# 28 adaLN chunks move from TensorE to VectorE; cached keys, bias tables and the out-projection's residual are handled in another order

## The chip, the cores and the metric

One core of one Trainium2 chip runs the whole program. The time is device microseconds of one launch. TensorE (PE) has two clock levels, 2.4 and 1.2 GHz; the profile gives the granted clock as a share of the higher one. The other engines are VectorE (DVE), ScalarE (ACT), GpSimd (POOL) and SyncE (SP); every DMA of this program is issued from SP's queue, in the order written, and a transfer that must wait for a buffer holds up all that stand behind it.

## The reference

Two layers (DEPTH = 2) over 128 context tokens and 512 latent tokens, width 1024. All arithmetic is fp32.

```python
for l in range(DEPTH):
    sh1, sc1, g1, sh2, sc2, g2 = split(silu(cond) @ ada_w[l] + ada_b[l], 6)      # adaLN, one row for context, one for latents
    h   = x * (1 + sc1) + sh1
    mix = concat([diff_attention(h), neighbourhood_attention(h), mlstm(h)])       # parts a, b, c of one input projection
    x   = layer_norm(ALPHA * x + g1 * (mix @ w_out[l]))
    h   = x * (1 + sc2) + sh2
    x   = layer_norm(ALPHA * x + g2 * (square(relu(h @ w_mlp1[l])) @ w_mlp2[l]))
```

The attentions of the latents also read 256 cached keys and values per head; part b adds a relative-position bias table to its local scores. `cond` has two rows (context and latents), so the adaLN product is 2 x 1024 by 1024 x 6144 for each layer.

## The kernel before, in words

The 640 tokens are five tiles of 128 (tile 0 context, tiles 1 to 4 latents). An fp32 product is three TensorE matmuls of two-part splits (`mul3`, L98 to L100): high x high, low x high, high x low. A weight comes from memory 1 MB at a time into one of two `raw` buffers (L208); ACT makes the high part (L170) and DVE the low part (L117), in four pieces each, into the slots `wt0`, `wt1` and, in the MLP, a third one in `AK`.

The program is a list of Units. The weight transfers are issued in the order of first use, as far ahead as the two buffers allow; a Unit that needs a weight makes sure that its split has been issued. A scheduler then settles the order on each engine from the order of the list.

A layer is: c_proj and c_attn (mLSTM), b_proj and b_attn (neighbourhood attention), a_proj and a_attn (differential attention), woven with the out-projection (`out_units`: for each tile the contributions of parts b and c, `cb`, and later those of part a, `a`, each in two halves of 512 columns), the norm, `put_T` (transpose, modulate, split), and the MLP (`mlp_units`: 8 blocks c of 512 hidden columns; the list has the up units of block c and then the down units of block c-1, one for each tile, each of which adds 128x1024 sums to `Y` on DVE, L1416).

The adaLN product is made in chunks of 1 MB (256 output columns), 24 for each layer, which share the `raw` buffers with the weights but are not split: 8 matmuls with the conditioning as the stationary operand (L368), a copy by ACT, and two Units later a "pick" of the two rows out of four groups. For v = 0, 1, 3, 4 (shifts and scales, wanted per partition) the pick is two matmuls against `sel2` (L385); for v = 2, 5 (the gates, wanted as rows) it is a matmul with `selr` (L380), a DVE add of a bias row that has its own DMA, and a DMA to `s_gate`. Where the chunks stand:

```python
ada = self.ada_units(l, (2, 3, 4))                            # in the attention of both layers, 12 chunks each
...
spare = self.ada_units(l, (5,))                               # in the MLP: 4 chunks in both layers
if more:
    spare += self.ada_units(l + 1, (0, 1)) + [self.mod_unit(l + 1, 0)]    # and 8 more in the first
for c in range(1, NFF - 1):
    P_ += ups[c]
    P_ += weave(downs[c - 1], spare[:2] if c < NFF - 2 else spare)
```

In part b each head's `prep` (L887 to L897) loads queries and keys, 128 KB of cached keys (`ckf`, L891, one buffer), which ACT and DVE split (L892, L893), and a bias table (`rw`, L896, one buffer). In `out_units`, `cb` multiplies its sums by the gate row (L1278), loads the residual's half tile (`z1`, two buffers), scales it in the second layer (L1283, L1284) and adds it (L1285); `a` multiplies its own sums by the gate (L1291) and adds them (L1292).

Of the kernel before, what the change touches and what calls it, by code (L numbers as in the profile page):

```python
# [42 lines left out]
PACK = (("abT", (DEPTH, 48)), ("lnT", (DEPTH, 4, KT)), ("ident", (P,)), ("sel2", (2,)), ("selr", (32,)),  # L43
# [25 lines left out]
class Step:  # L69
# [61 lines left out]
    def w_src(self, k):  # L131
        kind, l, j = k
        d = self.d
        if kind == "ada":
            return d["ada"][l, j]
# [43 lines left out]
    def run(self, plan):  # L179
# [32 lines left out]
        def try_split(slack=0):  # L212
            while state["split"] < state["dma"] and order[state["split"]][0] == "ada":
                state["split"] += 1
# [23 lines left out]
        for i, u in enumerate(plan):  # L238
# [3 lines left out]
            for k in u.w:  # L242
# [6 lines left out]
                if k[0] != "ada":  # L249
# [12 lines left out]
            for k in u.w:  # L262
                if k[0] == "ada" and last[k] == i:
                    del self.raw[k]
# [21 lines left out]
    def setup(self):  # L286
# [30 lines left out]
        nc.vector.tensor_tensor(self.condS, self.condS, e, ALU.mult)  # L317

# [39 lines left out]
    def ada_units(self, l, vecs, own=None):  # L358
# [15 lines left out]
        def pick(v, q, part):  # L374
            po = self.mm("pick")
            if v in (2, 5):
                ab = self.adp.tile([2, CW], F32, name="abrow", bufs=1)
                off = v * D + q * CW
                nc.sync.dma_start(ab, self.d["ada_b"][l, off:off + CW].partition_broadcast(2))
                nc.tensor.matmul(po[:32, :CW], self.selr, part, start=True, stop=True)  # L380
                nc.vector.tensor_tensor(ab, po[:2, :CW], ab, ALU.add)
                nc.sync.dma_start(self.s_gate[l][v // 3][:, q * CW:(q + 1) * CW], ab)
            else:
                for b in range(2):
                    nc.tensor.matmul(po[:, 2 * b:2 * b + 2], part[:, b * P:(b + 1) * P], self.sel2,  # L385
                                     start=True, stop=True)
                c0 = v * KT + 2 * q
                nc.vector.tensor_tensor(
                    self.adaF[l][:, v, 2 * q:2 * q + 2, :], po[:, :4].rearrange("p (a b) -> p a b", b=2),
                    self.abT[:, l, c0:c0 + 2, None].to_broadcast([P, 2, 2]), ALU.add)  # L390
# [4 lines left out]
        return out  # L395

# [173 lines left out]
    def head_load(self, l, kind, h):  # L570
# [4 lines left out]
        k = self.hp.tile([P, NTOK + PAST], F32R, name="hk", tag="hk", bufs=2)  # L575
        for g in range(2):
            o = slice(64 * g, 64 * g + 64)
            nc.sync.dma_start(q[o].bitcast(F32), self.s_q[kind + "q"][l][f][rows])
            nc.sync.dma_start(k[o, :NTOK].bitcast(F32), self.s_q[kind + "k"][l][f][rows, g])
# [274 lines left out]
    def b_proj(self, l):  # L854
# [13 lines left out]
        u = self.proj_fm(l, 4, self.sink_fm(l, "bq"))  # L868
        u += self.proj_fm(l, 5, self.sink_fm(l, "bk"))
        u += self.proj_tm(l, 6, range(NT), sink_v)  # L870
        return u

    def b_attn(self, l):
# [14 lines left out]
        def prep(h):  # L888
            q, k = self.head_load(l, "b", h)
            ck = self.bw.tile([P, PAST], F32, name="ckf", tag="ckf", bufs=1)  # L890
            nc.sync.dma_start(ck, d["cbk"][l, :, h])  # L891
            nc.scalar.activation(k[:, NTOK:], ck, AF.Copy, scale=0.125)  # L892
            nc.vector.scalar_tensor_tensor(k[64:, NTOK:], ck[64:], 0.125, k[64:, NTOK:].bitcast(F32),  # L893
                                           op0=ALU.mult, op1=ALU.subtract)
            rw = self.bw.tile([P, 8, 48], F32, name="rw", tag="rw", bufs=1)
            nc.sync.dma_start(rw, d["rpbw"][l, h])  # L896
            bm = []  # L897
            for v in range(3):
                b = self.bw.tile([P, 8, 32], F32, name="bm", tag="bm", bufs=4)
                o = 16 + BLK_OFF[v]  # L900
                nc.gpsimd.tensor_tensor(b, rw[:, :, o:o + 32], self.nmask[:, v, None, :].to_broadcast([P, 8, 32]), ALU.add)
                bm.append(b)
            hold[h] = (q, k, bm)
            hold[h, "r"] = self.bw.tile([P, 5], F32, name="br", tag="br", bufs=2)

        def scores(h, c):
# [9 lines left out]
            else:  # L916
# [3 lines left out]
                kl = k[:, P:NTOK].rearrange("p (r w) -> p r w", r=8)[:, :, w]  # L920
                self.mul2(ps[:, :256], kl, qq, stack_stationary=False)
                self.mul2(ps[:, 256:], k[:, NTOK:], qq, stack_stationary=False)
# [64 lines left out]
    def a_proj(self, l):  # L987
        nc, d = self.nc, self.d

        def op():  # L990
# [9 lines left out]
            nc.sync.dma_start(self.AV[:, 0:2], d["cav"][l])  # L1000

        held = {}

        def cached(g):
            if g < 4:
# [485 lines left out]
    def layer(self, l):  # L1491
# [75 lines left out]
        if more:  # L1567
            spare += self.ada_units(l + 1, (0, 1)) + [self.mod_unit(l + 1, 0)]
# [155 lines left out]
```

## Time and profile before

| | us |
|---|---|
| median of 3 runs | 1877.81 (1877.62 to 1882.55) |
| the profiled execution, its own time | 1881.12 |
| its span in the profile | 1879.3 |
| PE / DVE / ACT / POOL busy | 1790.4 / 1083.5 / 724.3 / 100.4 |
| TensorE's granted clock, mean | 0.981 |

The profile shows one execution. Busy times say how loaded an engine is over the whole span; what a stage is worth is read from the windows of that stage, from the chain of waits in it, and from the single rows of the timeline.

### The profile page before, as it was taken

Reading aid. Unit: us, or ns where it says so; the run is one execution under the profiler, and the core shown is the slowest. Engines: PE = TensorE matmul, PEld = TensorE weight load, DVE = VectorE, ACT = ScalarE, POOL = GpSimd, SP = SyncE. Lnnn points to the kernel's source line nnn. Section 1 sums busy time; section 2 is a strip of 40 time slices with the busy share of each in tenths; the row PEclk is TensorE's granted clock in tenths of the full one; section 3 lists DMA queues with packets and bytes.
Section 4 is the critical chain, followed back from the end, with each engine's and each line's share of the span. In section 5 each row is a group of like instructions: output and inputs, shape, how many; then the busy total and the mean of one; then the engine's idle time right before and its main releaser. Section 6 shows DMA issues by size and latency. Waiting matters only on the chain.

```text
span 1879.3 us, 29111 instructions
## 1 busy us (share of the span) xinstructions
PE 1790.4 (95%) x11666; PEld 1607.1 (86%) x11666; DVE 1083.5 (58%) x2068; ACT 724.3 (39%) x1640; POOL 100.4 (5%) x153
## 2 busy tenths in 40 slices
PE   6999999998999999999999989988989999999996
PEld 4999888887888888888899988877879889998895
DVE  4755566787623343345777645677977134544477
ACT  3343235456533231232364423353566223322220
POOL 1111100000000000000010210000010000000001
PEclk9999999999999999999999989989999999999998
DMA  9555465321423332333336655461214224222221
GB/s 352 163 165 163 164 201 189 111 85 57 146 68 102 123 115 91 109 107 140 106 116 222 162 167 179 145 214 64 85 45 146 90 90 157 69 90 68 75 94 56
DMA packets 82712, 239.23 MB, mean 127 GB/s; under 512 B 31808, under 2 KB 44544, under 8 KB 63888
## 3 DMA queue, kind: packets, MB, share of 16 engines
q1 hardware_dynamic: 82576, 237.36, 38.2%
q8 instruction: 92, 1.51, 0.3%
q14 instruction: 44, 0.36, 0.1%
HBM read 210.78 MB, written 26.55 MB: 126 GB/s over the span
## 4 chain that ended last, share of the span: by engine, by line
PE 82%; DVE 9%; DMA 5%; ACT 2%; issue 1%; SPq 1%; POOL 0%; DVEq 0%; ACTq 0%
PE m L98 15%; PE m L99 15%; PE m L100 15%; PE ss L98 7%; PE ss L99 7%; PE ss L100 7%; PE ss L1115 1%; PE m L1145 1%; PE m L961 1%; PE m L368 1%; DVE wt L117 1%; DMA ada<-ada 1%; DVE anm L1118 1%; DMA z<-s_x 1%; PE mz L106 1%
## 5 line engine op out<-in xcount | busy, mean ns | idle before, releaser
L98 PE MATMUL m<-wt,Th 128*128 128x256 f32 (+2 forms) x864 | 274.8, 319 | 7.1 <-DVE Tl L1206 2.8
L99 PE MATMUL m<-wt,Th 128*128 128x256 f32 (+2 forms) x864 | 269.1, 312 | 0.0
L100 PE MATMUL m<-wt,Tl 128*128 128x256 f32 (+2 forms) x864 | 267.0, 311 | 0.0
L98 PE MATMUL m<-Th,AK 128*128 128x384 f32 (+1 forms) x736 | 229.3, 312 | 4.9 <-DVE Th L112 4.2
L99 PE MATMUL m<-Tl,AK 128*128 128x384 f32 (+1 forms) x736 | 229.1, 312 | 0.9 <-DVE Tl L117 0.9
L100 PE MATMUL m<-Th,AK 128*128 128x384 f32 (+1 forms) x736 | 225.9, 311 | 0.0
L170 ACT ACTIVATE wt<-raw 128x512 fp32r<-128x512 f32 x244 | 146.7, 627 | 149.3 <-PE ss L100 85.6
L117 DVE TENSOR_TENSOR wt<-raw,wt 128x512 fp32r<-128x512 f32 x244 | 162.3, 693 | 47.1 <-ACT wt L170 46.2
L98 PEld LDWEIGHTS m<-wt,Th 128*128 128x128 f32 x864 | 168.6, 195 | 22.4 <-issue 5.5
L100 PEld LDWEIGHTS m<-wt,Tl 128*128 128x128 f32 x864 | 167.4, 195 | 10.8 <-issue 3.1
L99 PEld LDWEIGHTS m<-wt,Th 128*128 128x128 f32 x864 | 169.0, 196 | 7.6 <-issue 1.7
L98 PE MATMUL m<-Th,wt 128*128 128x384 f32 (+1 forms) x536 | 166.4, 311 | 0.0
L100 PE MATMUL m<-Th,wt 128*128 128x384 f32 (+1 forms) x536 | 166.2, 310 | 0.0
L99 PE MATMUL m<-Tl,wt 128*128 128x384 f32 (+1 forms) x536 | 165.9, 310 | 0.0
L1416 DVE TENSOR_TENSOR Y<-ss,Y 128x1024 f32<-128x1024 f32 x60 | 73.2, 1223 | 156.8 <-PE ss L100 156.8
L1390 DVE SCALAR_TENSOR_TENSOR rl<-m,rl 128x384 f32<-128x384 f32 (+1 forms) x128 | 62.2, 488 | 164.5 <-ACT rl L1389 164.5
L98 PEld LDWEIGHTS m<-Th,AK 128*128 128x128 f32 x736 | 140.7, 191 | 8.8 <-DVE Th L112 4.7
L99 PEld LDWEIGHTS m<-Tl,AK 128*128 128x128 f32 x736 | 140.7, 191 | 3.7 <-issue 1.6
L100 PEld LDWEIGHTS m<-Th,AK 128*128 128x128 f32 x736 | 140.5, 191 | 1.0 <-issue 0.8
L98 PE MATMUL ss<-wt,hid 128*128 128x512 f32 x356 | 139.7, 395 | 0.0
L1389 ACT ACTIVATE rl<-m 128x384 f32<-128x384 f32 (+1 forms) x128 | 55.3, 434 | 218.8 <-PE m L100 216.1
L99 PE MATMUL ss<-wt,hid 128*128 128x512 f32 x356 | 138.8, 391 | 0.0
(705 smaller groups left out, 3554.4 us busy)
## 6 DMA issues: line engine op xcount, KB each, us to landing
raw<-w SPq DMA_DIRECT2D x64, 1024.0 KB
raw<-ada SPq DMA_DIRECT2D x40, 1024.0 KB
raw<-w_in SPq DMA_DIRECT2D x24, 1024.0 KB
ada<-ada SPq DMA_DIRECT2D x8, 1024.0 KB
raw<-w_out SPq DMA_DIRECT2D x8, 1024.0 KB
s_x<-Y SPq DMA_DIRECT2D x15, 512.0 KB
hq<-s_cq SPq DMA_DIRECT2D x16, 320.0 KB
nb<-s_nm SPq DMA_DIRECT2D x16, 320.0 KB
```

The costliest lines, as they stand in the source:

```text
L98: mt(out, a[0], b[0], start=first, stop=False)
L99: mt(out, a[0], b[1], start=False, stop=False)
L100: mt(out, a[1], b[0], start=False, stop=last)
L106: self.nc.tensor.matmul(out, a, b, start=first and i == 0, stop=last and i == 1)
L117: self.nc.vector.tensor_tensor(out, x, hi.bitcast(F32), ALU.subtract)
L170: self.nc.scalar.activation(hi, r, AF.Copy)
L368: nc.tensor.matmul(ps[32 * g:32 * g + 32, :CW], self.condS[:, kt, :], raw[:, kt, :], start=kt % 2 == 0, stop=kt % 2 == 1)
L961: nc.tensor.matmul(out[64 * i:64 * i + 64], w, rhs, start=b == 0, stop=b == nb - 1)
L1115: nc.tensor.matmul(ps[:, b, :384], qq[i], K[:, j, b * 384:b * 384 + 384], start=i == 0, stop=i == 1)
L1389: nc.scalar.activation(r[:, :n], ps[:, :n], AF.Relu)
L1390: nc.vector.scalar_tensor_tensor(r[:, :n], ps[:, :n], 0.0, r[:, :n], op0=ALU.max, op1=ALU.mult)
L1416: nc.vector.tensor_tensor(y, ps, y, ALU.add)
```

## The change

1. **Chunks.** 28 chunks, v = 5 of the first layer and all 24 of the second, are made on DVE during the first layer's MLP (`ada_dve`). Their weights come transposed (`adaT`, prepared in memory): 128 output columns on the partitions, the 1024 inputs along the row, two such blocks in 1 MB. The silu of the conditioning is broadcast to all partitions (`condB`). Four instructions for each chunk (two blocks by two rows of cond) multiply and sum along the row. One chunk stands behind each of 28 down units. The second layer's attention and MLP have no chunks left.
2. **Gates.** All picks go by `sel2`; a gate is turned into rows once for each v (two transposes, an ACT copy, a DMA; `gate_rows`).
3. **Part b.** The cached keys of all four heads are one transfer of 512 KB and one split at the start of b_proj; bias tables have two buffers and are loaded two heads ahead, the `bm` tiles six buffers instead of four.
4. **Part a.** `cak` has two buffers, loaded a step earlier.
5. **Out-projection.** `cb` only copies its sums into `Y` (ACT). `a` adds, multiplies by the gate and adds the residual, which comes as whole rows of 1024, one tile ahead.
6. **Copies.** The second half of the `aT` copies (32 of 128x384) and one cast of each `put_T` (15 of 128x512) go from DVE to ACT.
7. **Start.** The conditioning is also loaded as rows, put through silu and stored (`s_cond`).

```diff
+    def ada_dve(self, l, vecs):
+        nc = self.nc
+        def emit(v, q):
+            raw = self.raw[("adt", l, 4 * v + q)].rearrange("p (a b) -> p a b", b=D)
+            for b in range(2):
+                for j in range(2):
+                    x = self.mw.tile([P, D], F32, name="adx", tag="z2", bufs=2)
+                    nc.vector.scalar_tensor_tensor(x, raw[:, b], 1.0, self.condB[:, j], op0=ALU.mult, op1=ALU.mult,
+                                                   accum_out=self.adaF[l][:, v, 2 * q + b, j:j + 1])
+            if q == 3:
+                a = self.adaF[l][:, v]
+                nc.vector.tensor_tensor(a, a, self.abT[:, l, KT * v:KT * v + KT, None].to_broadcast([P, KT, 2]), ALU.add)
+                if v in (2, 5):
+                    self.gate_rows(l, v)
+        return [Unit(0, lambda v=v, q=q: emit(v, q), (("adt", l, 4 * v + q),), soft=True) for v in vecs for q in range(4)]
...
-        ada = self.ada_units(l, (2, 3, 4))
+        ada = self.ada_units(l, (2, 3, 4) if l == 0 else ())
...
-        spare = self.ada_units(l, (5,))
+        spare = []
         if more:
-            spare += self.ada_units(l + 1, (0, 1)) + [self.mod_unit(l + 1, 0)]
+            spare = self.ada_dve(l, (5,)) + self.ada_dve(l + 1, (0, 1)) + [self.mod_unit(l + 1, 0)]
+            spare += self.ada_dve(l + 1, range(2, 6))
         for c in range(1, NFF - 1):
             P_ += ups[c]
-            P_ += weave(downs[c - 1], spare[:2] if c < NFF - 2 else spare)
-            spare = spare[2:]
+            for x in downs[c - 1]:
+                P_ += [x] + spare[:1]
+                spare = spare[1:]
...
+            ck = self.hp.tile([P, H, PAST], F32, name="ckf", tag="ckf", bufs=1)
+            nc.sync.dma_start(ck, d["cbk"][l])
+            k = self.BK = self.hp.tile([P, H, PAST], F32R, name="BK", tag="BK", bufs=1)
+            nc.scalar.activation(k, ck, AF.Copy, scale=0.125)
+            nc.vector.scalar_tensor_tensor(k[64:], ck[64:], 0.125, k[64:].bitcast(F32), op0=ALU.mult, op1=ALU.subtract)
...
         def cb(t, n):
             ps = self.out_mm(l, t, 2, n)
+            nc.scalar.activation(self.Y[:, t, 512 * n:512 * n + 512], ps, AF.Copy)
...
-            nc.vector.tensor_tensor(f, ps, self.g1[min(t, 1)][:, cols], ALU.mult)
-            nc.vector.tensor_tensor(self.Y[:, t, cols], self.Y[:, t, cols], f, ALU.add)
+            v, y, z = nc.vector, self.Y[:, t, cols], res[t][:, cols]
+            v.tensor_tensor(y, ps, y, ALU.add)
+            v.tensor_tensor(y, y, self.g1[min(t, 1)][:, cols], ALU.mult)
+            v.scalar_tensor_tensor(y, z, ALPHA if l == 0 else 1.0, y, op0=ALU.mult, op1=ALU.add)
```

DVE's order at the end of a middle block of the first MLP (c = 2), from the second down unit's add to the split of the next block's first weight (`ss` are a down unit's sums; `AK` is the third weight slot, `m1` the first up unit's sums). Before:

```order
L1416 TENSOR_TENSOR Y_99<-ss_6218,Y_99 128x1024
L1416 TENSOR_TENSOR Y_99<-ss_6257,Y_99 128x1024
L1416 TENSOR_TENSOR Y_99<-ss_6283,Y_99 128x1024
L381 TENSOR_TENSOR abrow_6310<-m3_6309,abrow_6310 2x256
L117 TENSOR_TENSOR AK_1981<-raw_6255,AK_1981 128x512 x2
L1416 TENSOR_TENSOR Y_99<-ss_6315,Y_99 128x1024
L117 TENSOR_TENSOR AK_1981<-raw_6255,AK_1981 128x512 x2
L1390 SCALAR_TENSOR_TENSOR rl_6389<-m2_6364,rl_6389 128x384
```

After, from the fourth down unit's add on (a chunk's four instructions are on L426):

```order
L426 SCALAR_TENSOR_TENSOR adx_6361,adaF1_99<-raw_6297,condB_5222 128x1024
L1483 TENSOR_TENSOR Y_110<-ss_6299,Y_110 128x1024
L426 SCALAR_TENSOR_TENSOR adx_6363,adaF1_99<-raw_6297,condB_5222 128x1024
L426 SCALAR_TENSOR_TENSOR adx_6365,adaF1_99<-raw_6297,condB_5222 128x1024
L426 SCALAR_TENSOR_TENSOR adx_6367,adaF1_99<-raw_6297,condB_5222 128x1024
L1483 TENSOR_TENSOR Y_110<-ss_6335,Y_110 128x1024
L117 TENSOR_TENSOR AK_1999<-raw_6333,AK_1999 128x512 x4
L1457 SCALAR_TENSOR_TENSOR rl_6406<-m1_6381,rl_6406 128x384
```

The next block's weight was split with two pieces ahead of the last add and two behind it; now all four pieces stand behind the last add, and so behind every chunk instruction of the block.

SP's queue at the start of the second layer's part b. Before, the cached keys of head 0 and its bias table stand behind the read-back of the values (`Y<-s_bv1`):

```order
L866 DMA s_bv1_129<-vb_10534 128x256
L208 DMA raw_10621<-ada 128x2048
L885 DMA Y_99<-s_bv1_129 128x1x256 x4
L891 DMA ckf_10579<-cbk 128x256
L896 DMA rw_10583<-rpbw 128x384
L1000 DMA AV_10550<-cav 128x1024
```

After, they are in the queue before the first part of the mLSTM's queries is stored:

```order
L1511 DMA s_x1_118<-Y_110 128x1024 x2
L910 DMA ckf_9749<-cbk 128x1024
L926 DMA rw_9754<-rpbw 128x384
L926 DMA rw_9756<-rpbw 128x384
L210 DMA raw_9344<-w_in 128x2048
L605 DMA s_cq10_123<-st_9187 128x1280
```

Some 45 rows of the queue lie between their new place and the read-back of the values.

## Rows read from the trace of the kernel before

**Rows 1.** the profile page, busy time of each engine and share of the span

```profile
PE 1790.4 (95%) x11666; PEld 1607.1 (86%) x11666; DVE 1083.5 (58%) x2068; ACT 724.3 (39%) x1640; POOL 100.4 (5%) x153
```

**Rows 2.** windows: us, busy of PE, PEld, DVE, ACT, POOL, clock, DMA share, GB/s

```profile
500.00:960.00 460.00, 459.88 (x2688) 406.03 (x2688) 218.44 (x353) 147.98 (x297) 5.19 (x12) 1.00 0.32 109
1095.00:1135.00 40.00, 33.13 (x257) 31.36 (x256) 17.93 (x39) 9.60 (x22) 6.61 (x10) 0.87 0.57 183
1135.00:1250.00 115.00, 111.18 (x983) 96.24 (x981) 73.75 (x179) 48.67 (x122) 3.56 (x6) 0.98 0.55 176
1250.00:1335.00 85.00, 72.03 (x398) 60.93 (x398) 68.14 (x131) 35.94 (x91) 2.41 (x4) 0.94 0.36 118
1480.00:1840.00 360.00, 360.00 (x2015) 322.50 (x2015) 167.51 (x250) 107.94 (x206) 0.00 (x0) 1.00 0.27 93
```

**Rows 3.** timeline of PE, one chunk in the first MLP: start, us, instruction

```profile
546.99 0.39 PE L100 MATMUL ss<-wt,hid 128*128 128x512 f32 x1
547.31 1.09 PE L368 MATMUL m<-raw,condS 128*32 128x256 f32 x16
548.33 0.50 PE L98 MATMUL ss<-wt,hid 128*128 128x512 f32 x1
548.67 0.40 PE L99 MATMUL ss<-wt,hid 128*128 128x512 f32 x1
548.91 0.40 PE L100 MATMUL ss<-wt,hid 128*128 128x512 f32 x1
```

**Rows 4.** timeline of PE, one pick of a gate's rows

```profile
559.47 0.62 PE L380 MATMUL m<-adpart,pack 128*32 128x256 f32 x2
560.02 0.44 PE L98 MATMUL m<-Th,AK 128*128 128x384 f32 x1
560.30 0.34 PE L99 MATMUL m<-Tl,AK 128*128 128x384 f32 x1
```

**Rows 5.** timeline of PE, one pick per partition

```profile
749.29 0.50 PE L385 MATMUL m<-pack,adpart 128*128 128x2 f32 x4
749.65 0.36 PE L98 MATMUL m<-Th,AK 128*128 128x256 f32 x1
749.86 0.28 PE L99 MATMUL m<-Tl,AK 128*128 128x256 f32 x1
```

**Rows 6.** groups by line and form: busy us, mean ns, idle before

```profile
L1416 DVE TENSOR_TENSOR Y<-ss,Y 128x1024 f32<-128x1024 f32 x60 | 73.2, 1223 | 156.8 <-PE ss L100 156.8
L117 DVE TENSOR_TENSOR wt<-raw,wt 128x512 fp32r<-128x512 f32 x244 | 162.3, 693 | 47.1 <-ACT wt L170 46.2
L1436 DVE SCALAR_TENSOR_TENSOR x<-Y,mv,lnrows 128x1024 f32<-128x1024 f32 x4 | 5.1, 1277 | 0.0
L1285 DVE SCALAR_TENSOR_TENSOR Y<-z,Y 128x512 f32<-128x512 f32 x20 | 13.7, 683 | 0.0
```

**Rows 7.** timeline of ACT, the read of an accumulator behind its activation

```profile
1142.76 0.20 ACT L925 ACTIVATION_READ_ACCUMULATOR bp<-my,bnm 128x1 f32 x1
```

**Rows 8.** timeline of DVE, the last down unit's add of two MLP blocks

```profile
626.01 1.22 DVE L1416 TENSOR_TENSOR Y<-ss,Y 128x1024 f32<-128x1024 f32 x1
...
866.93 1.23 DVE L1416 TENSOR_TENSOR Y<-ss,Y 128x1024 f32<-128x1024 f32 x1
```

**Rows 9.** one weight transfer alone: its issue on SP, and the windows behind

```profile
607.92 0.33 SPq L208 DMA_DIRECT2D raw<-w  x1
...
612.00:613.00 1.00, 1.00 (x6) 0.83 (x5) 0.00 (x0) 0.00 (x0) 0.00 (x0) 1.00 0.04 16
```

**Rows 10.** chain of waits, second layer, start of part b

```profile
1098.20 6.29 DMA Y<-s_bv
...
1108.96 7.55 DMA ckf<-cbk
```

**Rows 11.** chain of waits, second layer, start of the out-projection

```profile
1247.42 12.13 DMA lnrows<-ln
...
1267.90 6.85 DMA z<-s_x
```

More of the change, by code (lines that the diff above doesn't have):

```diff
@@ L212, in try_split @@
         def try_split(slack=0):
-            while state["split"] < state["dma"] and order[state["split"]][0] == "ada":
+            while state["split"] < state["dma"] and order[state["split"]][0] in ("ada", "adt"):
                 state["split"] += 1
@@ L262, in run @@
             for k in u.w:
-                if k[0] == "ada" and last[k] == i:
+                if k[0] in ("ada", "adt") and last[k] == i:
                     del self.raw[k]
@@ L375, in pick @@
             po = self.mm("pick")
[L376 to L390, printed above, removed]
+            for b in range(2):
+                nc.tensor.matmul(po[:, 2 * b:2 * b + 2], part[:, b * P:(b + 1) * P], self.sel2,
+                                 start=True, stop=True)
+            c0 = v * KT + 2 * q
+            nc.vector.tensor_tensor(
+                self.adaF[l][:, v, 2 * q:2 * q + 2, :], po[:, :4].rearrange("p (a b) -> p a b", b=2),
+                self.abT[:, l, c0:c0 + 2, None].to_broadcast([P, 2, 2]), ALU.add)
+            if v == 2 and q == 3:
+                self.gate_rows(l, v)
         for v in vecs:
@@ L395, in ada_units, with gate_rows, rows @@
         return out
+    def gate_rows(self, l, v):
+        nc = self.nc
+        def rows():
+            pt = self.mm("pick")
+            for j in range(2):
+                nc.tensor.transpose(pt[:KT, j * P:j * P + P], self.adaF[l][:, v, :, j], self.ident)
+            row = self.adp.tile([KT, 2, P], F32, name="grow", tag="adpart", bufs=2)
+            nc.scalar.activation(row, pt[:KT, :2 * P].rearrange("k (j p) -> k j p", j=2), AF.Copy)
+            nc.sync.dma_start(self.s_gate[l][v // 3].rearrange("j (k p) -> k j p", p=P), row)
+        self.defer(rows)
+    def ada_dve(self, l, vecs):
+        nc = self.nc
+        def emit(v, q):
+            raw = self.raw[("adt", l, 4 * v + q)].rearrange("p (a b) -> p a b", b=D)
+            for b in range(2):
+                for j in range(2):
+                    x = self.mw.tile([P, D], F32, name="adx", tag="z2", bufs=2)
[5 more added lines that the diff above has]
+                if v in (2, 5):
+                    self.gate_rows(l, v)
+        return [Unit(0, lambda v=v, q=q: emit(v, q), (("adt", l, 4 * v + q),), soft=True) for v in vecs for q in range(4)]
     def mod_unit(self, l, w):
@@ L1000, in op, with load @@
             nc.sync.dma_start(self.AV[:, 0:2], d["cav"][l])
+            for g in range(2):
+                load(g)
         held = {}
+        def load(g):
+            held[g] = self.at.tile([P, 2, PAST], F32, name="cak", tag="cak", bufs=2)
+            nc.sync.dma_start(held[g], d["cak"][l, :, 2 * g:2 * g + 2])
         def cached(g):
-            if g < 4:
-                held[g] = self.at.tile([P, 2, PAST], F32, name="cak", tag="cak", bufs=1)
-                nc.sync.dma_start(held[g], d["cak"][l, :, 2 * g:2 * g + 2])
             if g:
```

96 lines of the change are left out of this document (59 added, 37 removed).

## The prediction

> **What bounds the kernel now.** I read the busy times first: TensorE works 1790 of 1879 us and VectorE 1084 [rows 1]. Work taken from TensorE therefore counts nearly in full wherever TensorE is the engine that never rests, and VectorE has 795 us of room, though not necessarily at the right moments. The windows by stage tell where that holds [rows 2]. In the first MLP (500 to 960) and in the second (1480 to 1840) TensorE is busy to the last tenth of a microsecond; in the second layer's attention (1135 to 1250) it rests 4 of 115 us. At the start of the second layer's part b (1095 to 1135) it rests 7 of 40 us, and in the out-projection behind the attention (1250 to 1335) 13 of 85; in both the granted clock is below 1, at 0.87 and 0.94, so that some of the time runs at 1.2 GHz instead of 2.4. The chain of waits names what ends there last: the read-back of the values (6.29 us) and behind it, on the same queue, the cached keys (7.55) [rows 10]; in the out-projection the rows of the norm (12.13), then the half tiles of the residual (6.85 the first time) [rows 11].
>
> **What leaves TensorE.** A chunk: the matmul that should follow the one at 546.99 by 0.24 us starts 1.34 us behind it, and its own successor comes 0.34 behind instead of 0.24 [rows 3]. So a chunk costs 1.34 − 0.24 + 0.10 = 1.2 us. A gate's pick holds the next matmul for 0.55 us and slows it by about 0.1: 0.65 [rows 4]. A pick per partition holds it for 0.36 and slows it by about as much: 0.45 [rows 5]. 28 chunks, 12 gate picks and 16 others leave: 33.6 + 7.8 + 7.2 = 49 us. By stage: 12 chunks, 4 and 8 picks in the first MLP, 14.4 + 2.6 + 3.6 = 20.6; the same in the second layer's attention; 4 and 4 in the second MLP, 4.8 + 2.6 = 7.4.
>
> **What VectorE gets.** 112 instructions over 128x1024 that multiply and also sum along the row. The trace has none with a sum. The nearest row without one, of the same form and with two fp32 operands from SBUF, takes 1.28 us [rows 6]. ScalarE reads its accumulator out in a separate 0.20 us that overlaps the instruction ahead by about half [rows 7]. Bounds for one: 1.28 (the sum is free) and 2.55 (the sum takes as long as a second such instruction). I take 1.36, near the lower end, since the one accumulator row in the trace is that cheap. In all 152 us, on an engine that has the room; what counts is where in a block they stand.
>
> **The first MLP, block by block.** The last adds of the first and the fifth block lie 240.9 us apart [rows 8], four periods of 60.2 us. Each has two chunks and their picks, 3.5 us; without them a block is 56.7 us of TensorE alone, and six blocks are 340 instead of 361. VectorE in a block: 5 adds of 1.22 and 16 low parts of 0.69 [rows 6], 17.1, and 16 smaller steps of the squared ReLU; together about 25 (its whole rate in the MLP window, 218 of 460, would be 28.6 a block [rows 2]). Five chunks add 20 × 1.36 = 27. That makes 52 to 56 of 56.7: nearly full, so that what stands in the wrong order makes TensorE wait. In the new order 12 chunk instructions and 4 adds stand between the first down unit's add and the split of the next block's first weight. From that first add to the last low part VectorE needs 12 × 1.36 + 5 × 1.22 + 4 × 0.69 = 25.2 us, while TensorE, with 27 us for five down units, has 21.8 left after the first. So it waits for that weight by 3 to 5 us, also because the weight's transfer needs the buffer that a late chunk still holds, and such a transfer lands 4.1 us after its issue [rows 9]. Two chunk instructions ahead of the first add delay it as well: 2.9 us more, for the buffer of the sums. I placed the instructions of one block by hand with these durations and got waits of 2.9, 2.0 and 2.8: 56.7 + 7 = 63.5 or so for a block with five chunks. Blocks 2, 4 and 5 are such; block 3 has four chunks (59.5); in block 1 the sums are copied by ScalarE, and VectorE is not waited for (56); block 6, whose chunks share two buffers with the gated residual, 62. The sum, 368, is 7 us more than before. Bounds: no wait at all, −21; or VectorE the limit of every block with the order's waits on top, +21 at 1.7 us an instruction (4 × 66 + 2 × 59 = 382).
>
> **Part b.** With the keys and the first bias tables long in place, the 7.55 us fall out of the chain; the read-back of the values stays and is then the last. The wait is worth up to the 6.9 us of rest and the 5 us that a clock of 0.87 costs in 40 us [rows 2]: 0 to 12, taken as −9. The first layer has the same steps with a milder wait; half, −5 (0 to −9).
>
> **Second layer's attention.** 20.6 us leave. TensorE rests only 4 of 115 us there, but VectorE works 74 and ScalarE 49 in a chain of softmax steps, so that a part becomes rest: −16 (−8 to −21).
>
> **Out-projection.** `cb` then waits for ScalarE's copy alone; gate rows, norm rows and residual are needed only by `a`, one stage on. Of the 13 us of rest and the 5 us that the clock of 0.94 takes in 85 us, half: −9 (0 to −18). VectorE's work is not larger: three passes of 0.68 [rows 6] where five stood. In the first layer, which has no norm rows to wait for, −5 (0 to −9).
>
> **The rest.** Second MLP: −7, in full, since TensorE never rests there. At the start four small steps and a transfer ahead of the first chunks: +1 (0 to 2). The copies that move to ScalarE lie beside TensorE's work in the attention; in `put_T` cast and low part follow each other, +1 (0 to 3). The six `gate_rows` and the second buffer of `cak` I cost at nothing: a gate is needed a stage later; with that cover gone the transposes would be about 0.5 us each.
>
> The sum: 7 − 9 − 5 − 16 − 9 − 5 − 7 + 1 + 1 = −42. The profiled execution took 1881.1 by its own time, 1.8 more than its span and 3.3 above the median of the runs shown; 1881.1 − 42 = 1839, and from the median 1836. I say **1838 us**, with 1822 to 1857 as this case's own range.
>
> **Rivals.**
>
> *A. VectorE's chunks are hidden.* If the splits of the next weight come early enough, the blocks are at 56.7 us. Then the first MLP is 21 us shorter instead of 7 longer: 1838 − 28 = 1810. For it: VectorE's work fits into the block. Against it: the order shown at the block's end. Chance 0.18.
>
> *B. The new waits lower the clock.* Where TensorE rests in part, the trace has a lower granted clock: 0.94 at 85% busy, 0.87 at 83% [rows 2]. Blocks with 7 us of waiting in 63.5 are 89% busy. At 0.94, 56.7 us of work become 60.3, 3.6 more in each of six blocks: 1838 + 22 = 1860. Against it: in the attention 97% busy gave 0.98, and waits of 2 to 3 us are short. Chance 0.12.
>
> *C. The summing instruction takes twice as long (the other side).* At 2.55 us a block with five chunks is 25 + 20 × 2.55 = 76 us of VectorE alone, one with four 66: 4 × 76 + 2 × 66 = 436, 75 more than before. The other terms stay at −49: 1881 + 26 = 1907, slower. It decides from the point at which the six blocks take 49 us more, 68 us each: (68 − 25 − 7) / 18.7, about 1.9 us an instruction, where 7 are the waits of the order. For it speaks that no row has a sum; against it the 1.28 us with two SBUF operands and 1.22 with one from PSUM [rows 6], which show no price for the second operand. Chance 0.12. The Trainium skill, in "Vector Engine (DVE) Microarchitecture Reference", section "Points that are easy to get wrong", says that this instruction with two non-bf16 sources in SBUF runs at half throughput, because both read ports are taken. By that rule the sum would end at about 1907. The rows with two such sources at 1.28 us do not agree with it for the form without a sum; for the form with one no run here shows it yet.
>
> *D. The gains in the attention are swallowed.* If the softmax chain of VectorE and ScalarE is the real limit and the read-back of the values takes the place of the cached keys, part b, attention and out-projection give nothing: 7 − 7 + 2 = +2, about 1880, no change that can be measured. Against it: TensorE's 97% in the attention. Chance 0.08.
>
> **How the numbers follow.** Forecast 0.50, A 0.18, B 0.12, C 0.12, D 0.08. The measurement tells a change from none from about 0.3%, 5.6 us. Forecast, A and B are faster: 0.80; D the same, 0.08; C slower, 0.12. The range leaves C out and the tails of A and D: 1803 to 1878.
>
> **What would show it.** In the profile after: chunk instructions at 1.3 to 1.45 us (over 1.9: C). The six blocks of the first MLP 60 to 64 us apart, with TensorE resting some 5 us at the start of each, waiting for VectorE's low part of the third slot or for the sums' buffer; about 57 and no rest: A; a clock under 0.97 there: B. In the second layer's part b the cached keys gone from the chain; the attention stage some 16 us shorter, the second MLP 7. The prediction is wrong if the first MLP is not within 10 us of its old length or the second layer's attention stages together give less than 20.

## The result and the profile after

The changed kernel takes 1858.91 us (median of 4 runs, 1854.67 to 1864.66) against 1879.93 before: a ratio of 0.9888 (95% interval 0.9868 to 0.9907), 21 us faster. The forecast was 1838, 42 us faster: the direction holds and the size is half. The time lies 2 us above this case's own range (1822 to 1857) and inside the one with the rivals (1803 to 1878). The profiled execution is the slowest of the four, 1864.66 us, with a span of 1862.8, so that its stages add up to some 6 us more than the median.

The busy times answer to [rows 1]. TensorE lost 30 us where 49 were taken from it (47 in the kernel "with two bank turns" below, where it is busy 1743.4), and VectorE has 88 more (the chunks' rows cover 132, the other edits took the rest off it):

```profile
PE 1760.1 (94%) x11146; PEld 1598.5 (86%) x11146; DVE 1171.4 (63%) x2191; ACT 739.5 (40%) x1678; POOL 102.1 (5%) x153
```

Busy time can't tell where the time went, because a matmul at half clock is busy for twice as long. So I cut both spans at the same twelve events of the program and add one kernel from the experiments, the changed kernel with "two bank turns" (below):

| from the event before to ... | before | after | forecast change | measured | with two bank turns |
|---|---|---|---|---|---|
| 1. first mLSTM state matmul | 99.0 | 100.6 | +1 | +1.6 | 101.1 |
| 2. part b's first value matmul | 112.2 | 110.4 | −5 | −1.8 | 110.5 |
| 3. first squared ReLU of the MLP (part b, part a, out-projection) | 261.3 | 261.4 | −5 | +0.1 | 257.1 |
| 4. copy of the first down unit | 69.7 | 72.8 | +1 | +3.1 | 73.2 |
| 5. last down unit's add of block 6 | 368.6 | 357.9 | +7 | **−10.7** | 357.1 |
| 6. second layer's first state matmul | 106.2 | 108.5 | 0 | +2.3 | 108.5 |
| 7. part b's first value matmul | 111.5 | 120.9 | −9 | **+9.4** | 104.9 |
| 8. part a's first score matmul | 133.5 | 115.3 | −16 | −18.2 | 115.5 |
| 9. second MLP's first squared ReLU | 138.9 | 136.8 | −9 | −2.1 | 129.8 |
| 10. copy of its first down unit | 71.8 | 77.2 | 0 | +5.4 | 75.1 |
| 11. last down unit's add of block 6 | 348.9 | 343.6 | −7 | −5.3 | 343.6 |
| 12. end | 57.7 | 57.4 | 0 | −0.3 | 58.4 |
| span | 1879.3 | 1862.8 | −42 | −16.5 | 1834.8 |

Two terms have clearly the wrong sign. The windows of the stages 5, 7, 8, 9 and 11 in the changed kernel (columns as in [rows 2]), and last the 20.5 us inside stage 7 at half clock:

```profile
545.20:903.10 357.90, 349.49 (x1891) 310.46 (x1891) 266.39 (x442) 99.32 (x196) 0.00 (x0) 1.00 0.45 154
1011.60:1132.50 120.90, 112.88 (x790) 110.07 (x790) 64.63 (x151) 44.74 (x121) 19.51 (x27) 0.89 0.53 150
1132.50:1247.80 115.30, 108.68 (x881) 99.85 (x879) 74.73 (x182) 52.08 (x132) 2.57 (x4) 0.97 0.39 117
1247.80:1384.60 136.80, 122.06 (x712) 109.08 (x712) 105.68 (x183) 87.35 (x214) 11.29 (x18) 0.94 0.19 60
1461.80:1805.40 343.60, 343.60 (x1871) 308.29 (x1870) 151.16 (x221) 100.03 (x186) 0.00 (x0) 1.00 0.22 74
1050.90:1071.40 20.50, 20.50 (x97) 20.31 (x96) 7.51 (x20) 7.91 (x22) 3.58 (x5) 0.50 0.32 83
```

In the first MLP (first row) the clock is 1.00 throughout and TensorE rests 8.4 of 357.9 us. In stage 7 (second row) the clock is 0.89, with 112.9 us busy for fewer matmuls than before. The window of the same stage in the kernel before:

```profile
1017.00:1128.50 111.50, 104.63 (x805) 101.75 (x805) 61.89 (x147) 44.66 (x120) 19.52 (x25) 0.95 0.60 174
```

**Stage 5.** The chunk's instruction, grouped by line, answers to the rows with two SBUF operands in [rows 6]; the read of the sum is a second instruction:

```profile
L426 DVE SCALAR_TENSOR_TENSOR adx<-raw,condB 128x1024 f32<-128x1024 f32 x112 | 132.0, 1221 | 22.8 <-DMA raw<-adaT 22.4 <-DVE Y L1483 0.4
L426 DVE DVE_READ_ACCUMULATOR adx<-raw,condB 128x1 f32 x112 | 9.4, 84 | 0.0
```

The timeline of VectorE at the end of a block shows what a row's length does not: each instruction starts 0.08 before the one ahead ends, and the 0.08 read lies in that overlap. A chunk's instruction costs 1.14 to 1.15 us from start to start, not 1.36.

```profile
728.46 1.22 DVE L426 SCALAR_TENSOR_TENSOR adx<-raw,condB 128x1024 f32<-128x1024 f32 x1
729.61 0.08 DVE L426 DVE_READ_ACCUMULATOR adx<-raw,condB 128x1 f32 x1
729.61 1.22 DVE L426 SCALAR_TENSOR_TENSOR adx<-raw,condB 128x1024 f32<-128x1024 f32 x1
730.75 0.09 DVE L426 DVE_READ_ACCUMULATOR adx<-raw,condB 128x1 f32 x1
730.75 1.22 DVE L1483 TENSOR_TENSOR Y<-ss,Y 128x1024 f32<-128x1024 f32 x1
731.89 1.22 DVE L426 SCALAR_TENSOR_TENSOR adx<-raw,condB 128x1024 f32<-128x1024 f32 x1
...
741.09 1.22 DVE L1483 TENSOR_TENSOR Y<-ss,Y 128x1024 f32<-128x1024 f32 x1
742.23 2.49 DVE L117 TENSOR_TENSOR AK<-raw,AK 128x512 fp32r<-128x512 f32 x4
```

The last adds of a block start at 625.4, 683.7, 741.1, 799.5 and 858.0: 58.2 us a block, where 60.2 stood and 59.5 to 63.5 were forecast. What TensorE waits for in all of stage 5 (view of the waits: total, times, longest):

```profile
PE ss L98 <- DVE Y L1483: 4.7, 5, 1.1
PE m L100 <- DVE AK L117: 2.2, 3, 0.8
PE ss L99 <- DVE AK L117: 0.8, 1, 0.8
PE m L98 <- ACT AK L172: 0.7, 1, 0.7
```

These are the two waits of the forecast, the sums' buffer and the next block's weight, at 0.9 and 0.7 a block instead of 2.9 and 4.8.

**Stage 7.** The stage has two pieces: the mLSTM up to its last product with its state, and from there part b's start. The first took 73 us before and takes 87 now; the second took 38 and takes 33. So part b did get shorter, and the loss is in the mLSTM. Its window before, and in the changed kernel:

```profile
1017.00:1090.30 73.30, 73.30 (x561) 71.31 (x560) 43.70 (x107) 34.65 (x98) 13.26 (x16) 1.00 0.57 160
...
1011.60:1099.10 87.50, 85.04 (x575) 82.41 (x575) 45.30 (x110) 36.16 (x101) 12.64 (x18) 0.88 0.49 137
```

The timeline of TensorE shows a wait of 2.46 us for a DMA in front of head 2's product with the mLSTM state, and the chain of waits shows the same four matmuls of a head at 0.39 us ahead of it and at 0.85 behind it:

```profile
1047.18 0.28 PE L99 MATMUL m<-Tl,wt 128*128 128x256 f32 x1
1049.93 0.30 PE L98 MATMUL m<-Cst,hq 128*128 128x130 f32 x1 [2.46 <-DMA hq<-s_cq]
```

```profile
1036.91 0.39 PE mx L826 x4
...
1053.35 0.85 PE mx L826 x4
```

SP's timeline shows what stands ahead of the queries `hq`: stores of the new state (`new_n<-so` is the last), then a weight (`raw<-w_in`) that waits for a free buffer from 1029.1 to 1033.6, then the row `nb`, which waits for its own:

```profile
1028.49 0.62 SPq L870 DMA_DIRECT2D new_n<-so  x1
1033.65 0.34 SPq L210 DMA_DIRECT2D raw<-w_in  x1
1034.27 3.09 SPq L770 DMA_DIRECT2D nb<-s_nm  x2
1037.45 0.69 SPq L605 DMA_DIRECT2D s_bq<-st  x1
1038.23 0.67 SPq L617 DMA_DIRECT2D hq<-s_cq  x1
```

No edit is aimed at the mLSTM. In the kernel before, stores and weight stood behind the first of the queries, and `hq` was issued at 1030.8, 13.8 us after the stage's start; here it is 26.6 us after it.

### The profile page after: what moved, and what is told of

It reads as the page before. It is cut to its first block, busy times and chain, and to the rows that moved or that the text cites. A ratio compares the mean times of both kernels' runs of the same rounds, so it can differ in the third digit from the quotient of the medians.

```text
span 1862.8 us, 28136 instructions
## 1 busy us (share of the span) xinstructions
PE 1760.1 (94%) x11146; PEld 1598.5 (86%) x11146; DVE 1171.4 (63%) x2191; ACT 739.5 (40%) x1678; POOL 102.1 (5%) x153
## 4 chain that ended last, share of the span: by engine, by line
PE 78%; DVE 10%; DMA 6%; ACT 4%; issue 1%; POOL 0%; SPq 0%; DVEq 0%; ACTq 0%
PE m L98 15%; PE m L100 15%; PE m L99 15%; PE ss L98 6%; PE ss L99 6%; PE ss L100 6%; DVE adx L426 3%; PE m L1201 2%; PE ss L1171 2%; ACT pf L1399 2%; PE m L1012 1%; DVE Y L1483 1%; DMA hq<-s_bq 1%; PE m L824 1%; PE m L1194 1%
## 5 line engine op out<-in xcount | busy, mean ns | idle before, releaser
L98 PE MATMUL m<-wt,Th 128*128 128x256 f32 (+2 forms) x864 | 274.2, 318 | 10.7 <-DVE AK L117 2.4
L117 DVE TENSOR_TENSOR wt<-raw,wt 128x512 fp32r<-128x512 f32 x252 | 167.9, 695 | 83.3 <-ACT wt L172 81.8
L98 PE MATMUL m<-Th,AK 128*128 128x384 f32 (+1 forms) x672 | 210.5, 314 | 9.0 <-ACT Th L110 8.3
L99 PE MATMUL m<-Tl,AK 128*128 128x256 f32 (+1 forms) x672 | 209.8, 313 | 0.4 <-DVE Tl L117 0.4
L100 PE MATMUL m<-Th,AK 128*128 128x256 f32 (+1 forms) x672 | 207.9, 313 | 2.2 <-DVE AK L117 2.2
L98 PE MATMUL m<-Th,wt 128*128 128x256 f32 (+1 forms) x600 | 186.9, 312 | 0.8 <-DVE Y L1353 0.8
L100 PE MATMUL m<-Th,wt 128*128 128x256 f32 (+1 forms) x600 | 186.2, 311 | 0.1
L99 PE MATMUL m<-Tl,wt 128*128 128x256 f32 (+1 forms) x600 | 186.3, 311 | 0.0
L426 DVE SCALAR_TENSOR_TENSOR adx<-raw,condB 128x1024 f32<-128x1024 f32 x112 | 132.0, 1221 | 22.8 <-DMA raw<-adaT 22.4
L98 PE MATMUL ss<-wt,hid 128*128 128x512 f32 x356 | 141.0, 396 | 4.7 <-DVE Y L1483 4.7
L100 PE MATMUL ss<-wt,hid 128*128 128x512 f32 x356 | 140.4, 394 | 0.0
L99 PE MATMUL ss<-wt,hid 128*128 128x512 f32 x356 | 140.3, 394 | 0.0
L98 PEld LDWEIGHTS m<-Th,AK 128*128 128x128 f32 x672 | 128.2, 191 | 11.3 <-ACT Th L110 8.7
L172 ACT ACTIVATE AK<-raw 128x512 fp32r<-128x512 f32 x140 | 85.3, 628 | 132.3 <-PE ss L100 88.8
L1483 DVE TENSOR_TENSOR Y<-ss,Y 128x1024 f32<-128x1024 f32 x60 | 73.2, 1222 | 93.5 <-PE ss L100 93.5
```

The lines of the kernel that those rows point to most:

```text
L98: mt(out, a[0], b[0], start=first, stop=False)
L99: mt(out, a[0], b[1], start=False, stop=False)
L100: mt(out, a[1], b[0], start=False, stop=last)
L117: self.nc.vector.tensor_tensor(out, x, hi.bitcast(F32), ALU.subtract)
L172: self.nc.scalar.activation(hi, r, AF.Copy)
L426: nc.vector.scalar_tensor_tensor(x, raw[:, b], 1.0, self.condB[:, j], op0=ALU.mult, op1=ALU.mult, accum_out=self.adaF[l][:, v, 2 * q + b, ...
```

## The experiments

Each kernel is the changed one with the edit shown, unless it says otherwise; times are medians, and all ratios are to the kernel before, measured beside each.

**The changed kernel again, with no edit.**

> The changed kernel once more, unchanged, beside the three others. Theory 1 (the loss in the second layer's mLSTM belongs to the program: TensorE waits 2.5 us there for a head's queries, and the half clock of some 20 us behind it follows from that): 1855 to 1865 us, and the profile again shows a wait for the queries near 1047 us with about 20 us of half clock behind it. Theory 2 (that half clock is chance): the same median, but a profile without it and a span near 1850.

1859.18 us (1854.35 to 1865.0), ratio 0.9888 (0.987 to 0.9906). The profile has a wait for the queries again, of 1.7 us, and 20.5 us of half clock at 1048.4 to 1068.9: theory 1. Both profiles are of the slowest execution of their run; that the half clock is as long in those near 1855 is not shown.

**Chunks back on TensorE, other edits kept.**

```diff
-            spare = self.ada_dve(l, (5,)) + self.ada_dve(l + 1, (0, 1)) + [self.mod_unit(l + 1, 0)]
-            spare += self.ada_dve(l + 1, range(2, 6))
+            spare = self.ada_units(l, (5,)) + self.ada_units(l + 1, (0, 1)) + [self.mod_unit(l + 1, 0)]
...
-        ada = self.ada_units(l, (2, 3, 4) if l == 0 else ())
+        ada = self.ada_units(l, (2, 3, 4))
```

> The changed kernel with the 28 chunks back on TensorE at the places they had, all other edits kept (gates still by two transposes). Theory 1 (the chunks are what made the kernel faster; the other edits nearly cancel each other): 1880 to 1888, some 25 us slower than the changed kernel: 9 in the first MLP, 12 to 15 in the second layer's attention, 5 in the second MLP. Theory 2 (the chunks on VectorE are worth little and the other edits carry the gain): 1858 to 1866.

1892.85 us, ratio 1.0063 (1.0042 to 1.0084): 34 us slower than the changed kernel, more than theory 1 had, and 13 slower than before. The chunks carry more than the whole gain; the other edits together lose.

**put_T's first cast back on VectorE.**

```diff
-            self.copy("A", self.Th[:, t, 4 * b:4 * b + 4], f)
+            self.copy("DA"[b], self.Th[:, t, 4 * b:4 * b + 4], f)
```

> The changed kernel with one edit undone: in put_T the first half's cast is VectorE's again. Theory 1 (the cast on ScalarE, priced at +1, makes TensorE wait at the start of both MLPs: 8.2 us in two waits, where it was 4.2): 4 to 8 us faster than the changed kernel, the longest wait for the cast back at about 2 us. Theory 2 (the wait only takes the place of another in the same chain): within 2 us of the changed kernel.

1846.57 us, ratio 0.9816 (0.9803 to 0.9828): 12.6 us faster, more than either theory said. The waits explain the smaller part. The changed kernel's row, and then that of this one:

```profile
PE m L98 <- ACT Th L110: 8.3, 2, 4.3
```

```profile
PE m L98 <- DVE Th L112: 4.2, 2, 2.1
```

That is 4 us, less 3 for another wait that grew (VectorE's low part in front of the out-projection's matmuls, 5.4 instead of 2.1). Another 6 came in stage 9 (130.9 us instead of 136.8), where its own order differs too. A comparison without the loss of stage 7 follows below.

**The weight held behind the queries on SP's queue.**

```diff
-                self.nc.sync.dma_start(r, src)
+                i = self.nc.sync.dma_start(r, src).ins
+                for q in self.behind:
+                    self.tc.add_manual_dep(i, q.name, mybir.DependencyInfo(
+                        mybir.DependencyClass.NoSync, mybir.DependencyReason.DATA), reason="queue")
+                self.behind = []
...
+            self.behind = self.loads if (l, h) == (1, 2) else []
```

(`loads` are the two query transfers of the head; the next weight, and no other, is put behind them.)

> The changed kernel with one weight transfer of the second layer held behind the mLSTM's queries of head 2 on SP's queue. Theory 1 (the weight ahead of them holds the queue until a buffer is free, the queries come late, TensorE waits and then runs 20 us at half clock): the wait of 2.5 us is gone, and 5 to 13 us with it: 1846 to 1854. Theory 2 (the queries are late for another reason, or the clock falls there anyway): 0 to 3 us.

1843.36 us, ratio 0.9804 (0.9791 to 0.9817): 15.8 us faster, a little above the range of theory 1. Stage 7 is 108.7 us, 12 less, its clock 0.97; stage 9 is 6.5 shorter as well, and why is not shown:

```profile
1009.30:1118.00 108.70, 104.76 (x789) 101.44 (x789) 61.89 (x149) 44.48 (x120) 19.62 (x27) 0.97 0.56 156
```

The mechanism of theory 1 does not come out, though. The queries are issued no earlier (26.2 us after the stage's start instead of 26.6), because other rows hold the queue as long (5.1 us in front of `s_bq`). The same matmul waits nearly as long, now for VectorE; what is shorter is the half clock behind it, 3.4 us:

```profile
1046.15 0.30 PE L98 MATMUL m<-Cst,hq 128*128 128x130 f32 x1 [1.97 <-DVE t L851]
```

So the weight is not what makes the queries late. Why the half clock is shorter without it in front is not shown.

**Where the queue's order comes from.** The order of the programs shows it: in the four that undo one edit (chunks, cast, part a's keys, part b's keys) the weight stays ahead of the queries each time. What the gates bring to the attention is one more request for a PSUM bank (`gate_rows`, through `mm`, which gives banks out in turn: y, z, w, y, ...). From there on each later turn is one further, and the second layer's mLSTM state sums stand in bank y, which the scores use, where they stood in w. With that turn completed to a full round, SP's order there is the old one again. Of the changed kernel:

```
L210 DMA raw_10154<-w_in 128x2048
L770 DMA nb_9928<-s_nm1_142 128x640 x2
L605 DMA s_bq11_132<-st_9971 128x1280
L617 DMA hq_9922<-s_cq11_124 64x1280
```

With the two turns added:

```
L619 DMA hq_9922<-s_cq11_124 64x1280
L772 DMA nb_10181<-s_nm1_142 128x640
L620 DMA hk_10176<-s_ck11_128 64x640
L607 DMA s_bq11_132<-st_9971 128x1280
L210 DMA raw_10154<-w_in 128x2048
```

**Two bank turns.**

```diff
             pt = self.mm("pick")
+            if self.single:
+                self.turns["yzw"] += 2
```

> The changed kernel with one line more: where a gate is turned into rows during the first layer's attention, the turn by which PSUM banks are given out is moved on by two, so that all later turns are what they were before the change. No instruction is added. Theory 1 (that extra turn put the second layer's mLSTM state sums into a bank that its scores use as well, the scheduler then placed a weight ahead of the queries, and 2.5 us of waiting with 20 us at half clock came of it): 1840 to 1850, no wait for the queries in that stage. Theory 2 (the bank has no part in it): 1855 to 1865.

1836.69 us, ratio 0.977 (0.9755 to 0.9784): 22 us faster than the changed kernel, more than theory 1 had, with no work added or taken away. Stage 7 takes 104.9 us at clock 0.98 and has no wait for `hq`; its mLSTM takes 73.1 us, as before the change. Stage 9 is shorter as well, so that not all of the 22 us lies in the mLSTM:

```profile
1007.50:1112.40 104.90, 102.67 (x789) 100.31 (x789) 64.12 (x151) 45.47 (x121) 21.18 (x27) 0.98 0.58 163
...
1227.90:1357.70 129.80, 118.19 (x705) 104.73 (x706) 104.71 (x183) 83.12 (x203) 10.80 (x18) 0.96 0.18 59
```

**One bank turn in the kernel before.**

```diff
             po = self.mm("pick")
+            if (l, v, q) == (0, 2, 3):
+                self.turns["yzw"] += 1
```

> The kernel before with one extra turn of the PSUM banks in the first layer's attention and nothing else changed. Theory 1 (the extra turn alone makes the loss in the second layer's mLSTM): 10 to 18 us slower than before, 1889 to 1897, with the wait for the queries and the long half clock in its profile. Theory 2: within 3 us of before.

1877.23 us, ratio 0.9987 (0.9977 to 0.9997): 3.5 us faster than the kernel before, a miss for theory 1. The wait for the queries comes, and stage 7 grows from 111.5 to 117.3 us, but without the long half clock (3.4 us), and the turns behind it shorten other stages by as much:

```profile
PE m L98 <- DMA hq<-s_cq: 2.5, 1, 2.5
```

So the turn makes the late queries; what follows from them depends on what else is in the program. In this one they cost the mLSTM 6 us and the whole nothing.

**Part a's cached keys late.**

```diff
-            for g in range(2):
-                load(g)
...
-            held[g] = self.at.tile([P, 2, PAST], F32, name="cak", tag="cak", bufs=2)
+            held[g] = self.at.tile([P, 2, PAST], F32, name="cak", tag="cak", bufs=1)
...
+            if g < 4:
+                load(g)
...
-                if g < 3:
-                    load(g + 1)
```

> The changed kernel with the fourth edit undone: the cached keys of part a have one buffer and are loaded a step later. Theory 1 (loaded early, they stand on ScalarE ahead of part b's first exponentials and take the place of the bias table as the last thing waited for: a wait of 6 us by the profile of the first layer): 3 to 6 us faster than the changed kernel. Theory 2 (the read-back of the values ends no earlier, so that the wait only changes its name): within 2 us.

1857.34 us, ratio 0.988 (0.9864 to 0.9897): 1.8 us, within the spread, as theory 2 had it. In its profile the wait of the first chunk of part b for ScalarE's exponential is 4.4 us instead of 5.7.

**Part b's cached keys and bias tables loaded by each head, as before.**

```diff
+            ck = self.bw.tile([P, PAST], F32, name="ckf", tag="ckf", bufs=1)
+            nc.sync.dma_start(ck, d["cbk"][l, :, h])
...
+            rw = self.bw.tile([P, 8, 48], F32, name="rw", tag="rw", bufs=1)
+            nc.sync.dma_start(rw, d["rpbw"][l, h])
```

> The changed kernel with the third edit undone: each head's cached keys and its bias table are loaded in its own prep, as before. Theory 1 (the edit shortens the start of part b, priced at 5 and 9 us; in the trace the first layer gained 2 and the second some 8): 8 to 12 us slower than the changed kernel. Theory 2 (the read-back of the values is what ends last, and the edit is worth nothing): within 3 us.

1852.78 us, ratio 0.9858 (0.9842 to 0.9874): 6 us *faster*, against both theories. Stage 2 is 3.7 us longer than in the changed kernel's second profile (114.5 against 110.8), as the edit's worth would be; stage 7 is 113.7 against 120.2, because here, too, the half clock of 20 us is missing, though the wait for the queries is there (2.1 us). The run shows again that this loss swamps the terms beside it. Part b's own piece of stage 7, behind the mLSTM, is 36.1 us instead of 33.4: there the edit is worth 2.7.

The last four kernels all have the two bank turns; they are compared with 1836.69.

**Chunks back on TensorE**, by the diff of the second experiment.

> The changed kernel with the two bank turns added and the 28 chunks back on TensorE. Theory 1 (chunks are worth some 33 us on VectorE, with or without the loss in the mLSTM): 1867 to 1874, that is 30 to 36 us above the kernel with the turns alone (1836.7), 12 of them in the first MLP, 17 in the second layer's part b and attention projections, 5 to 8 in the second MLP; all other edits together then give 7 to 13 us. Theory 2 (with the loss gone TensorE has slack, and the chunks' place matters less): below 1860.

1876.55 us, ratio 0.9984 (0.9974 to 0.9995). This is a little above theory 1. The chunks are worth 40 us: 13.6 in stage 5, 15.4 in stage 8, 8.7 in stage 11, the rest at the MLPs' starts and in stage 9. All other edits together, with the two turns, are worth 2.5. Stage 5 of this kernel, with nearly as little rest as before the change:

```profile
541.20:911.90 370.70, 370.19 (x2121) 321.42 (x2120) 155.44 (x246) 104.92 (x206) 0.00 (x0) 1.00 0.32 109
```

**Out-projection as before.** The functions `cb` and `a` are the old ones again:

```diff
-            nc.scalar.activation(self.Y[:, t, 512 * n:512 * n + 512], ps, AF.Copy)
+            nc.vector.tensor_tensor(y, ps, self.g1[min(t, 1)][:, cols], ALU.mult)
...
-            v.tensor_tensor(y, ps, y, ALU.add)
+            nc.vector.tensor_tensor(f, ps, self.g1[min(t, 1)][:, cols], ALU.mult)
+            nc.vector.tensor_tensor(self.Y[:, t, cols], self.Y[:, t, cols], f, ALU.add)
```

> The changed kernel with the two bank turns added and the out-projection's edit undone. Theory 1 (the edit is worth what the stage shows, 6 us in the first layer and 13 in the second): 1850 to 1857. Theory 2 (the stage grew shorter for another reason, the order and the clock): 1836 to 1842.

1840.59 us, ratio 0.9789 (0.977 to 0.9808): the edit is worth 3.9 us, inside the range of theory 2 (1836 to 1842) and far from theory 1: 3.3 in stage 3, 2.6 in stage 9, less 2.0 at the second MLP's start, where the old order is shorter.

**The cast back on VectorE**, by the diff above.

> The changed kernel with the two bank turns added and put_T's cast back on VectorE. Theory 1 (the cast's 4 us of extra waiting at the starts of the two MLPs are real): 1830 to 1834. Theory 2 (the 12.6 us that undoing the cast gave without the turns came from the order and the clock in the second layer alone): 1836 to 1839.

1831.72 us (four runs, 1830.68 to 1838.71), ratio 0.975 (0.9727 to 0.9772): 5 us, in the range of theory 1. This is the fastest kernel of the study, 47 us below before. Its profiled execution is the slowest of the four, so its stages are not read closely; in it the wait for the cast falls by 4.6 us, that for the low part in front of the out-projection grows by 3.6, and the MLPs' starts are no shorter. Where the 5 us come from is not shown.

**The cast back, and part a's keys late**, by the two diffs above.

> The changed kernel with the two bank turns added, put_T's cast back on VectorE and part a's cached keys loaded late as before. Theory 1 (the three are separate losses): 1827 to 1833, the fastest of all. Theory 2 (the late load of the cached keys gives its 2 us only because the order around it changes): within 2 us of the kernel with turns and cast.

1836.35 us, ratio 0.9768 (0.9749 to 0.9787): 4.6 us slower than with the early load, against both theories. Its waits have one that the kernel with the early load lacks, in stage 7:

```profile
PE m L98 <- DVE AV L1076: 4.6, 1, 4.6
```

With the mLSTM mended the early load is worth keeping.

## Why the prediction was right, and where it failed

**What bounds the kernel** holds. Work taken from TensorE in stages 5, 8 and 11 came back as time: 40 us between the kernels with and without it (both with the two turns), beside a count of 49 in prices of rows.

**The first MLP, block by block: the step that was mis-sized.** "+7" was −10.7. The mechanism was right, both waits are there. The price was wrong in two places. The instruction costs 1.14 us from start to start instead of 1.36: the forecast added lengths of rows, which overlap by 0.08, and added the accumulator's read on top, which lies in that overlap. Over the 12 instructions at a block's end that is 2.6 us of the 25.2 that VectorE was said to need; the adds and low parts, priced by length too, take off another 0.7 (5 × 0.08, and 2.49 for four low parts instead of 2.76). So VectorE needs some 22 (22.1 in the block shown), and TensorE has 21.8. The hand placement, made with the longer prices, turned a near tie into 7 us of waiting a block (its three waits even add up to 7.7); 1.7 were measured. By the marks that the prediction set for itself it is wrong here: the stage changed by 10.7 where 10 was the limit, and the instruction, 1.22, is below the 1.3 to 1.45 that it named. The other mark, 20 from the second layer's attention stages, is just met by stages 8 and 9 (20.3) and missed if stage 7 is counted with them (10.9).

**Part b, "−9" in the second layer, and the `gate_rows` at nothing: the step that failed.** In part b's own piece the change gave −4.9, and −6.5 with the two turns; the cached keys are out of the chain, and that edit alone is worth 2.7 there (one profile each). The term was too large, but its sign is right. What turned the stage to +9.4 is +14.2 in the mLSTM ahead of it, for which the sum has no term. The prediction priced the six `gate_rows` at nothing, because a gate is needed a stage later. That looks at the gate's data; what cost time is the PSUM bank that one of them asks for, a resource given out in turn, by which one edit's extra request reached another layer's mLSTM. The order of the changed program has the queries behind the stores and the weight, and could be read ahead of the result; no edit names that place.

The ten profiles side by side, one execution each (times in us; "issued" counts from the stage's start, "half clock" is the stretch that begins within about 1 us of that wait's end):

| kernel | queries issued | wait at head 2's product | half clock | mLSTM's piece | part b's piece |
|---|---|---|---|---|---|
| before | 13.8 | none | none | 73.2 | 38.2 |
| two bank turns | 13.8 | none | none | 73.1 | 31.8 |
| changed | 26.6 | 2.5 | 20.5 | 87.5 | 33.4 |
| changed, again | 26.7 | 1.7 | 20.5 | 86.7 | 33.5 |
| chunks on TensorE | 26.2 | 2.3 | 20.5 | 87.3 | 34.4 |
| cast on VectorE | 26.2 | 2.0 | 20.5 | 87.0 | 33.8 |
| part a's keys late | 26.4 | 2.3 | 10.2 | 82.5 | 33.2 |
| part b's keys by head | 26.2 | 2.1 | none | 77.5 | 36.1 |
| before, one turn | 26.2 | 2.5 | 3.4 | 79.6 | 37.7 |
| weight held behind | 26.2 | 2.0, for VectorE | 3.4 | 77.3 | 31.4 |

Shown: that the turn makes the queries late. All five kernels with the round completed issue them at 13.8 and take 73.1 us for the mLSTM; the kernel before with one turn put in issues them at 26.2. Shown as well: that the long half clock is the larger part of the loss where it comes (half of 20.5 is 10.3 of the 14.2 us, the wait another 2.5). Not settled: what decides how long the half clock is. Waits of 1.7 to 2.5 us are followed by 20.5, 10.2, 3.4 us or none, and the shortest of them by 20.5; the length of the wait does not decide it.

**Second layer's attention, "−16":** −18.2, of which the chunks alone give 15.4. **Second MLP, "−7":** −5.3 between its blocks; the chunks alone give 8.7.

**Out-projection, "−9" and "−5":** 3.9 us together by the experiment. The half that was taken of its rest and its clock was too much. VectorE and ScalarE are busy 105.7 and 87.4 of the 136.8 us of stage 9, which fits what rival D said of the softmax steps; no run tries it. VectorE's passes were miscounted as well: "three where five stood" leaves out the scaling of the residual, which stays in the second layer; there five passes stand where six stood, and in the first layer three where four stood.

**First layer's part b, "−5":** −1.8. The edit itself is worth 3.7 there, by the kernel that loads by head. The early load of part a's keys may have taken some of it: the kernel that loads them late is 1.2 to 1.6 us shorter in that stage, and by the chain of waits they are the last to land, with ScalarE's copy of them in front of part b's first exponentials. With turns and cast the late load makes no difference there (109.4 and 109.2), so this is not shown.

**put_T, "+1":** 3.1 and 5.4 us at the MLPs' starts, and 5 in the total for the cast by the medians. What stage 10 lost stays open in the main: the old out-projection takes off 2.0, and the `aT` copies, the other half of that edit, were not tried alone.

**The rivals.** A, hidden chunks, is nearly what the first MLP did: 58.2 us a block where it said 56.7. B, the lower clock, named the right size (1860) and the wrong place: the first MLP's clock is 1.00, and the half clock came in the mLSTM. C, twice the time for the sum, falls with the row of 1221 ns, where the add with one source in PSUM takes 1222. The Trainium skill's "Vector Engine (DVE) Microarchitecture Reference", section "Points that are easy to get wrong", says that two non-bf16 sources in SBUF halve this instruction's throughput; the trace does not agree with it, by the same two rows. That the total came within 2 us of B's number, and the kernel with the two turns within 2 of the forecast, is in good part luck: too dark a first MLP stood against too bright an out-projection and MLP start.

## What to carry to other kernels

Price a run of instructions by the distance from start to start in the timeline, not by the mean length of a row; here 16% in the price stood between 1.7 us of waiting a block and 7. After a change to anything that is given out in turn (PSUM banks, buffers), compare the order on every engine and DMA queue in all stages, not only in those of the edits: one more turn in the first layer lengthened the second layer's mLSTM by 14 us, and one line that completes the round made the kernel 22 us faster. The same turn put into the kernel before cost nothing in total, so the order has to be read and measured each time. And when several edits come together, take the loss out first and then price the others: with it in, undoing an edit that shortens its own stages by 3.7 and 2.7 us looked like a gain of 6.

## What the runs showed of the hardware

Waits of 1.7 to 2.5 us on TensorE were followed by 20.5 us at 1.2 GHz in three programs (the changed kernel, twice, and those with the chunks or the cast undone; 1050.9 to 1071.4 in the first), at full busy share during that time, and by 10.2 us, 3.4 us or none in others with nearly the same work. A wait that costs 2.5 us in the view of the waits can so come with a loss of 14. VectorE's multiply with a sum along the row is one instruction of 1221 ns and a read of 84 ns, and the read adds nothing to the distance between two of them (1.14 to 1.15 us).
